# Feed-forward kernel, first product: two token groups inside the inner-dimension loop, in two PSUM banks, with one stationary tile

## The chip, the cores and the metric

The kernel runs on one core of a Trainium2 chip. The metric is the device time of one execution in microseconds, the median of several runs. One core has a matrix engine (PE in the profile, with its weight loads listed apart as PEld), a vector engine (DVE), a scalar engine (ACT), a general one (POOL), and a sync engine whose queue (SP) starts most DMAs. Each engine works through its own instructions in order; engines wait for one another by semaphores. Matrix products are accumulated in PSUM, which has eight banks here, each a tile of 128 partitions by 512 float32 numbers.

## The reference, cut to what matters

One step of a diffusion backbone with one layer, over 1280 tokens: 1024 sample tokens and 256 prompt tokens, with D = 1024 columns and an inner width of 4096 in the feed-forward part.

```python
u = rmsnorm(x, g_norm1) * (1 + sc1) + sh1
proj = u @ w_in                      # pooling, gating, q/k/v/o, gates
y_a = pool_branch(xp, ...)           # centred means, minus x, per-group linear map
y_b = sgu_branch(su, sv, ...)        # chunks of 128 positions
y_c = mlstm_branch(q, k, v, ...)     # 4 heads, forward and backward scans
merged = sum_r sigmoid(gate_r) * (y_r @ w_branch[r])
x = x + gt1 * (merged @ w_out)
u2 = rmsnorm(x, g_norm2) * (1 + sc2) + sh2
x = x + gt2 * (jnp.square(jax.nn.relu(u2 @ w_ff1)) @ w_ff2)
y = rmsnorm(x, g_final)
```

## The kernel before

**Tiling.** Tokens stand in three groups (GROUPS): group 0 and group 1 with 512 sample tokens each, group 2 with the 256 prompt tokens. A product keeps its accuracy by splitting both operands into a high and a low part and doing three matmuls per inner step: high by high, high by low, low by high. The function `dense` (L117 to L125) does so for one group of tokens: for each of eight inner steps k it issues L123 and L124, which share the weight slice `whi[:, s]` as the stationary operand, and L125 with `wlo[:, s]`. All eight steps accumulate in one PSUM tile.

**PSUM.** The eight banks are shared out between two rings of tiles: `ps_mm` (L75, 3 banks) for projections and for the first feed-forward product, and `ps_sd` (L78, 5 banks) for nearly all else: the mLSTM heads, the pooling branch's product (L683), the chunk mixing (L704) and the second feed-forward product. A tile can be written again once its last reader is done.

**What sets the order.** The program is written stage by stage, but the tile framework's scheduler places each instruction: it estimates when operands and buffers come free, and moves ready work ahead. So one stage's matmuls stand among another's, and what stands where on PE depends on the PSUM rings, too. On the chip each engine then keeps that order and only waits.

**The stages in time**, by the profile's clock: start and conditioning to about 130 us, mLSTM heads to about 451, pooling branch and the start of the gating branch to about 525, gated branch outputs and output projection to about 1240, feed-forward to the end.

**Heads and pooling.** A head's last product per token tile is `pv` (L561, L563); DVE and ACT normalise it (L566 to L577), and L580 makes `yc`. After the last head its scratch space `z` is used by the pooling branch: POOL clears parts of it (L630 to L635), for each of four channel groups (3, 2, 1, 0) a projection `xp` is copied out of PSUM (L641), windowed sums run over `z` on DVE and POOL (`winsum`, L663), are multiplied by the inverse counts (L670, L674) and reduced by `xp` (L681); then PE does `pp` (L683), and L686 and L687 split the result. The projections for `xp` and for the gating branch `su` are made by `dense` and depend on none of that. L617 normalises the rows `vn` of the gating branch, which stand in the same stretch of DVE.

**Feed-forward** (L859 to L942). Sixteen blocks `fb`, each with two inner tiles `f` of 128 of the 4096 inner columns. `ff_in(g, f)` makes the first product of one group with one inner tile (`dense` into `ps_mm`), then relu (L871) and square (L873) on ACT, square and difference (L874, L875) on DVE. `ff_out(g)` adds the block's part of the second product, per token tile and half of the columns: six matmuls (L888 to L890) into `ps_sd`, multiplied by `gt2` (L897) and added to the rows `xt` (L898) on DVE. In the last block part of these go to a temporary on DVE (L894) and are added on POOL (L895), then rows are normalised, scaled (L903) and written out (L905, L907). The weights come through `load_w` (L86): a DMA, the high part by ACT (L93), the low part by DVE (L94), with three buffers for each part.

Of the kernel before, what the change touches and what calls it, by code (L numbers as in the profile page):

```python
# [35 lines left out]
class Pinned:  # L36
    """Engine whose instructions stay in program order."""

# [11 lines left out]
def hybrid_step(  # L50
# [21 lines left out]
    def tmp(name, dt=F32):  # L72
        return tp.tile([P, 512], dt, tag="t", name=name)

    def ps_mm(name):  # L75
        return pp.tile([P, 512], F32, tag="mm", name=name, bufs=3)

    def ps_sd(name):  # L78
        return pp.tile([P, 512], F32, tag="sd", name=name, bufs=5)

# [73 lines left out]

    # RMSNorm, modulation and transpose of a group of tokens
    def norm_rows(x, n, name):
# [38 lines left out]

    # conditioning: SiLU, then shift1 and scale1 as columns
    scond = cp.tile([P, KT, 2], F32, name="scond")
# [106 lines left out]

    # gate pre-activations
    bgt = cp.tile([36, 2], F32, name="bgt")
# [110 lines left out]

    # remaining modulation rows: shares of the vector engine, summed over partitions on GpSimd
    macc = []
# [26 lines left out]

    # one mLSTM head
    knat = z[:, 0:1280].rearrange("p (c t) -> p c t", t=P)
# [144 lines left out]

    # normalised rows for the spatial gating branch
    vn = []
# [22 lines left out]

    # pooling branch
    wpt = z[:, 7200:7712].rearrange("p (g c) -> p g c", c=P)  # L620
# [69 lines left out]

    # spatial gating branch
    wst = z[:, 9216:9728].rearrange("p (g c) -> p g c", c=P)
# [30 lines left out]

    # gated branch outputs, summed
    zoff = (0, 4096, 8192)
# [41 lines left out]

    # output projection and residual
    mT = [[] for _ in range(KT)]
# [31 lines left out]
    def modulate_ff(g):  # L801
        t0, n = GROUPS[g]
        tiles = range(t0 // P, (t0 + n) // P)
        fs = small([P, 4], f"fs{g}")[:, : len(tiles)]
        V.reduce_sum(fs, fsq[:, tiles[0] : tiles[-1] + 1, :], axis=mybir.AxisListType.X)
        r = rstd_of(fs, len(tiles), f"f{g}")
        # normalised rows are made a quarter of the columns at a time, so that little room is needed
        j = 1 if g == 2 else 0
        for qt in range(4):
            xn = []  # L810
            for ii, i in enumerate(tiles):
                if ii % 2 == 0:
                    t = tmp(f"xn{i}_{qt}")
                v = t[:, (ii % 2) * 256 : (ii % 2) * 256 + 256]
                xv = xt[i][:, qt * 256 : (qt + 1) * 256]
                if ii % 2 == 0:
                    A.activation(v, xv, AF.Copy, scale=r[:, ii : ii + 1])
                else:
                    V.tensor_scalar(v, xv, r[:, ii : ii + 1], None, ALU.mult)
                xn.append(v)  # L820
            for kk in range(2):
                k = qt * 2 + kk
                ps = ps_sd(f"pt2{g}_{k}")
                for ii in range(n // P):
# [26 lines left out]

    # feed-forward
    gt2 = bcast_rows(3 * D, "gt2")
# [6 lines left out]
    for fb in range(NFF // FB):  # L860
# [4 lines left out]

        def ff_in(g, f):
            n = GROUPS[g][1]
            ps = ps_mm(f"f1_{fb}_{f}_{g}")
            dense(ps, w1[f], u2, g)
            t = tmp(f"re{f}_{g}")  # L870
            A.activation(t[:, :n], ps[:, :n], AF.Relu)  # L871
            part = split_part(f"h{f}", g)
            A.activation(part[0], t[:, :n], AF.Square)  # L873
            V.tensor_tensor(t[:, :n], t[:, :n], t[:, :n], ALU.mult)  # L874
            V.tensor_tensor(part[1], t[:, :n], part[0].bitcast(F32), ALU.subtract)  # L875
            hid[f].append(part)

# [45 lines left out]

        # a group's rows start the first block as soon as they are ready,
        # and in the last one are finished under the products of the next group
        if fb == 0:
            order = [(g, f) for g in range(3) for f in range(FB)]
        elif last:
            order = [(g, f) for f in range(FB) for g in range(2)]
            load_w2()  # L930
        else:
            order = [(g, f) for f in range(FB) for g in range(3)]
        for g, f in order:
            ff_in(g, f)
        if not last:
            load_w2()
        ff_out(0)
        if last:
            for f in range(FB):
                ff_in(2, f)  # L940
        ff_out(1)
# [103 lines left out]
```

## Time and profile before

| what | value |
|---|---|
| times of three runs | 2095.59, 2093.40, 2092.47 us |
| median | 2093.4 us |
| span of the profiled execution, first to last instruction | 2092.1 us |
| mean granted PE clock over the span | 0.993 |
| ACT busy | 581.7 us (28%) |
| POOL busy | 229.3 us (11%) |
| data moved | 142.74 MB, 68 GB/s on average |

The profile's page gives a span and no separate time for the profiled execution; the span is 1.3 us below the median of the runs and 0.4 us below the fastest. A window of the trace lists, for a stretch of time, how long each engine was busy, with the number of its instructions, the mean clock granted to PE (1.00 is full speed) and the share of DMA time. A row of the timeline gives the start, the length, engine and line, operation, output and inputs, and in brackets the idle time before it with what ended it. A PE row's length includes the pipeline's drain: where one matmul starts right behind another, the distance between two starts is what it costs.

### The profile page before, as it was taken

The numbers are of one execution on the slowest core, as the hardware profiler recorded it, in microseconds if no ns is written. First come the engines' busy times: TensorE is split into PE (matmuls) and PEld (weight loads), VectorE is DVE, ScalarE is ACT, GpSimd is POOL, SyncE is SP. The second block draws the span as 40 slices with busy tenths as digits, with TensorE's granted clock in tenths as the row PEclk, the third lists the DMA queues.
The fourth block names the chain that finished last, engine by engine and source line by source line (L and its number), as shares of the span: only waits on it lengthen the run. The fifth ranks groups of instructions, "written<-read, shape, count | busy, mean of one in ns | idle before, by whom it ended". The sixth has DMA issues, their size and how long they took to land.

```text
span 2092.1 us, 27452 instructions
## 1 busy us (share of the span) xinstructions
PE 2039.9 (98%) x11120; PEld 1758.5 (84%) x11120; DVE 1243.9 (59%) x2075; ACT 581.7 (28%) x1210; POOL 229.3 (11%) x207
## 2 busy tenths in 40 slices
PE   6999999998999999999999999999999999999996
PEld 3788888996888888888899988888888888888885
DVE  6674444458543345445253687666666666666777
ACT  6534454643111111111132431111111111111113
POOL 2000001037022222122010100000000000000004
PEclk9999999999999999999999999999999999999998
DMA  8011111124122343252141111111111111111102
GB/s 314 21 33 54 42 58 46 39 66 161 56 73 79 97 156 91 71 182 75 48 151 41 55 37 41 41 41 41 41 41 41 41 41 39 33 41 41 41 21 101
DMA packets 56479, 142.74 MB, mean 68 GB/s; under 512 B 6944, under 2 KB 12960, under 8 KB 56352
## 3 DMA queue, kind: packets, MB, share of 16 engines
q1 hardware_dynamic: 45568, 122.03, 18.6%
q10 hardware_dynamic: 7488, 11.02, 1.4%
q0 software_dynamic: 3296, 7.94, 1.3%
q8 instruction: 87, 1.43, 0.3%
q14 instruction: 40, 0.33, 0.1%
HBM read 124.67 MB, written 16.29 MB: 67 GB/s over the span
## 4 chain that ended last, share of the span: by engine, by line
PE 93%; DVE 3%; issue 1%; POOL 1%; DMA 1%; ACT 1%; SPq 0%; DVEq 0%; POOLq 0%; ACTq 0%
PE f L124 7%; PE f L123 7%; PE f L125 7%; PE f L888 7%; PE f L889 7%; PE f L890 7%; PE br L123 5%; PE br L124 5%; PE br L125 5%; PE pb L756 3%; PE pb L758 3%; PE pb L757 3%; PE po L841 2%; PE po L842 2%; PE po L843 2%
## 5 line engine op out<-in xcount | busy, mean ns | idle before, releaser
L897 DVE TENSOR_TENSOR f<-f,gt 128x512 f32<-128x512 f32 x305 | 211.1, 697 | 42.1 <-PE f L890 42.1
L898 DVE TENSOR_TENSOR z<-z,f 128x512 f32<-128x512 f32 x305 | 207.3, 684 | 7.3
L93 ACT CAST hi_f<-raw_f 128x1024 fp32r<-128x1024 f32 x63 | 64.6, 1049 | 462.7 <-PE f L889 417.4
L874 DVE TENSOR_TENSOR re<-re 128x512 f32<-128x512 f32 (+1 forms) x96 | 57.4, 599 | 165.9 <-ACT h1h L873 116.8
L751 ACT ACTIVATE sg<-br 128x512 f32<-128x512 f32 (+1 forms) x72 | 37.9, 526 | 300.8 <-PE br L125 287.6
L895 POOL TENSOR_TENSOR z<-z,fo 128x512 f32<-128x512 f32 x15 | 20.4, 1367 | 849.7 <-DVE fo L894 848.1
L871 ACT ACTIVATE re<-f 128x512 f32<-128x512 f32 (+1 forms) x96 | 50.4, 526 | 196.2 <-PE f L125 196.1
L889 PE MATMUL f<-hi_f,h0l 128*128 128x512 f32 x256 | 99.7, 390 | 0.0
L890 PE MATMUL f<-lo_f,h0h 128*128 128x512 f32 x256 | 99.6, 389 | 0.0
L888 PE MATMUL f<-hi_f,h0h 128*128 128x512 f32 x256 | 99.1, 390 | 0.0
L94 DVE TENSOR_TENSOR lo_f<-raw_f,hi_f 128x1024 fp32r<-128x1024 f32 x63 | 77.0, 1222 | 31.0 <-ACT hi_f L93 30.9
L888 PE MATMUL f<-hi_f,h1h 128*128 128x512 f32 x240 | 93.4, 389 | 0.0
L889 PE MATMUL f<-hi_f,h1l 128*128 128x512 f32 x240 | 93.4, 389 | 0.0
L436 DVE SCALAR_TENSOR_TENSOR acc<-wb,scond,acc 128x512 f32<-128x512 f32 x112 | 82.2, 791 | 18.2 <-DMA wb<-in_w_ada 18.2
L890 PE MATMUL f<-lo_f,h1h 128*128 128x512 f32 x240 | 92.7, 389 | 0.0
L443 POOL PARTITION_ALL_REDUCE acc<-acc x16 | 54.3, 3435 | 324.2 <-DVE acc L436 290.0
L765 DVE TENSOR_TENSOR sg<-pb,sg 128x512 f32<-128x512 f32 (+1 forms) x48 | 28.7, 599 | 100.8 <-PE pb L758 95.9
L763 DVE TENSOR_TENSOR z<-pb,sg 128x512 f32<-128x512 f32 (+1 forms) x24 | 14.4, 600 | 78.9 <-PE pb L758 78.9
L890 PEld LDWEIGHTS f<-lo_f,h0h 128*128 128x128 f32 x256 | 48.1, 188 | 10.0
L889 PEld LDWEIGHTS f<-hi_f,h0l 128*128 128x128 f32 x256 | 48.1, 188 | 9.3
L888 PEld LDWEIGHTS f<-hi_f,h0h 128*128 128x128 f32 x256 | 48.1, 188 | 9.3
L94 DVE TENSOR_TENSOR lo_br<-raw_br,hi_br 128x1024 fp32r<-128x1024 f32 x24 | 37.2, 1551 | 28.9 <-ACT hi_br L93 28.8
(1656 smaller groups left out, 6271.3 us busy)
## 6 DMA issues: line engine op xcount, KB each, us to landing
raw_f<-in_w_ff SPq DMA_DIRECT2D x64, 512.0 KB, 3.7
wb<-in_w_ada SPq DMA_DIRECT2D x32, 512.0 KB, 4.0
raw_br<-in_w_in SPq DMA_DIRECT2D x24, 512.0 KB, 3.6
wa<-in_w_ada SPq DMA_DIRECT2D x32, 256.0 KB, 5.4
raw_wb<-in_w_branch SPq DMA_DIRECT2D x12, 512.0 KB, 3.6
z<-in_xs SPq DMA_DIRECT2D x10, 512.0 KB, 7.2
z<-in_xs POOLq DMA_DIRECT2D x10, 512.0 KB, 4.8
out_y<-z SPq DMA_DIRECT2D x9, 512.0 KB, 2.6
```

Source lines behind the costliest of these rows:

```text
L93: A.copy(hi, raw)
L94: eng.tensor_tensor(lo, raw, hi.bitcast(F32), ALU.subtract)
L123: PE.matmul(ps[:, :n], whi[:, s], ahi, start=k == 0, stop=False)
L124: PE.matmul(ps[:, :n], whi[:, s], alo, start=False, stop=False)
L125: PE.matmul(ps[:, :n], wlo[:, s], ahi, start=False, stop=k == KT - 1)
L436: V.scalar_tensor_tensor(acc[j], wa[:, k2, :], scond[:, k, j : j + 1], acc[j], ALU.mult, ALU.add)
L756: PE.matmul(pb[:, :n], wb[0][:, s], yh, start=kc == 0, stop=False)
L888: PE.matmul(ps, hh[:, o : o + P], whi, start=f == 0, stop=False)
L889: PE.matmul(ps, hl[:, o : o + P], whi, start=False, stop=False)
L890: PE.matmul(ps, hh[:, o : o + P], wlo, start=False, stop=f == FB - 1)
L897: V.tensor_tensor(ps, ps, gt, ALU.mult)
L898: V.tensor_tensor(xt[i][:, s], xt[i][:, s], ps, ALU.add)
```

## The change

`ff_in` no longer takes one group but a tuple of groups, and no longer calls `dense`. For each inner step k it goes over the three operand pairs, and inside over the groups: with the tuple (0, 1) the same stationary slice is used twice in a row, for group 0 into one bank and for group 1 into another. In blocks 1 to 14 the order is groups (0, 1) together and then group 2, for each inner tile; in the first block the groups stay single, and in the last block (0, 1) together come first and group 2 after `ff_out(0)`, as before. So that two tiles of the first product can be open at once, `ps_mm` has four banks in place of three, and `ps_sd` four in place of five. Comments were taken out. The number and the sizes of the matmuls, and all work on the other engines, are the same.

```diff
     def ps_mm(name):
-        return pp.tile([P, 512], F32, tag="mm", name=name, bufs=3)
+        return pp.tile([P, 512], F32, tag="mm", name=name, bufs=4)
     def ps_sd(name):
-        return pp.tile([P, 512], F32, tag="sd", name=name, bufs=5)
+        return pp.tile([P, 512], F32, tag="sd", name=name, bufs=4)
...
-        def ff_in(g, f):
-            n = GROUPS[g][1]
-            ps = ps_mm(f"f1_{fb}_{f}_{g}")
-            dense(ps, w1[f], u2, g)
-            t = tmp(f"re{f}_{g}")
-            A.activation(t[:, :n], ps[:, :n], AF.Relu)
...
+        def ff_in(gs, f):
+            ps = {g: ps_mm(f"f1_{fb}_{f}_{g}") for g in gs}
+            whi, wlo = w1[f]
+            for k in range(KT):
+                s = slice(k * P, (k + 1) * P)
+                for w, part, first, end in ((whi, 0, k == 0, False), (whi, 1, False, False), (wlo, 0, False, k == KT - 1)):
+                    for g in gs:
+                        PE.matmul(ps[g][:, : GROUPS[g][1]], w[:, s], u2[k][g][part], start=first, stop=end)
+            for g in gs:
+                n = GROUPS[g][1]
+                t = tmp(f"re{f}_{g}")
+                A.activation(t[:, :n], ps[g][:, :n], AF.Relu)
...
         if fb == 0:
-            order = [(g, f) for g in range(3) for f in range(FB)]
+            order = [((0,), f) for f in range(FB)] + [((1,), f) for f in range(FB)] + [((2,), f) for f in range(FB)]
         elif last:
-            order = [(g, f) for f in range(FB) for g in range(2)]
+            order = [((0, 1), f) for f in range(FB)]
             load_w2()
         else:
-            order = [(g, f) for f in range(FB) for g in range(3)]
+            order = [(gs, f) for f in range(FB) for gs in ((0, 1), (2,))]
...
             for f in range(FB):
-                ff_in(2, f)
+                ff_in((2,), f)
```

The rings of PSUM banks serve the whole program, so the scheduler's placement changes outside the feed-forward part as well. Three places on PE show it. In these rows the output stands first, then the moving operand and the stationary one, or for `pv` and `pp` the like; a name ends in a running number, `f1_9_0_1` is block 9, inner tile 0, group 1, and `p_xp11` is the projection `xp` of channel group 1 for token group 1.

**First place: the feed-forward part, block 9**, the start of its first product. Before:

```order
L123 MATMUL f1_9_0_0_14108<-u20h0_10095,hi_f1_18_14098 128x512
L124 MATMUL f1_9_0_0_14108<-u20l0_10096,hi_f1_18_14098 128x512
L125 MATMUL f1_9_0_0_14108<-u20h0_10095,lo_f1_18_14099 128x512
L123 MATMUL f1_9_0_0_14108<-u21h0_10105,hi_f1_18_14098 128x512
L124 MATMUL f1_9_0_0_14108<-u21l0_10106,hi_f1_18_14098 128x512
L125 MATMUL f1_9_0_0_14108<-u21h0_10105,lo_f1_18_14099 128x512
L123 MATMUL f1_9_0_0_14108<-u22h0_10121,hi_f1_18_14098 128x512
```

After:

```order
L873 MATMUL f1_9_0_0_14108<-u20h0_10095,hi_f1_18_14098 128x512
L873 MATMUL f1_9_0_1_14109<-u20h1_10316,hi_f1_18_14098 128x512
L873 MATMUL f1_9_0_0_14108<-u20l0_10096,hi_f1_18_14098 128x512
L873 MATMUL f1_9_0_1_14109<-u20l1_10317,hi_f1_18_14098 128x512
L873 MATMUL f1_9_0_2_14172<-u20c_10476,hi_f1_18_14098 128x256 x2
L873 MATMUL f1_9_0_0_14108<-u20h0_10095,lo_f1_18_14099 128x512
L873 MATMUL f1_9_0_1_14109<-u20h1_10316,lo_f1_18_14099 128x512
L873 MATMUL f1_9_0_0_14108<-u21h0_10105,hi_f1_18_14098 128x512
```

Before, the tile of group 0 is filled step by step, and the tile of group 1 later; now the two tiles alternate, each stationary slice standing twice in a row, and a few matmuls of group 2 stand between them. Counted over the program, 903 pairs of neighbouring 512-column matmuls of the first product now share the stationary slice and differ in the bank; before there were 3.

**Second place: the end of the last mLSTM head**, where PE does the last `pv` tiles (`pv3_8`, `pv3_9`) among projections. Before:

```order
L123 MATMUL p_xp32_4460<-u6c_806,hi_xp3_4402 128x256
L124 MATMUL p_xp32_4460<-u6c_806,hi_xp3_4402 128x256
L561 MATMUL pv3_8_3764<-z_80,w3_2_0_3744 128x129
L561 MATMUL pv3_9_3775<-z_80,w3_2_0_3744 128x129
L563 MATMUL pv3_9_3775<-z_80,e3_2_0_3749 128x129
L125 MATMUL p_xp32_4460<-u6c_806,lo_xp3_4403 128x256
L561 MATMUL pv3_8_3764<-z_80,w3_2_1_3755 128x129
L561 MATMUL pv3_9_3775<-z_80,w3_2_1_3755 128x129
```

After:

```order
L123 MATMUL p_xp11_4708<-u3h1_683,hi_xp1_4677 128x512
L124 MATMUL p_xp11_4708<-u3l1_684,hi_xp1_4677 128x512
L561 MATMUL pv3_8_3764<-z_80,w3_2_0_3744 128x129
L561 MATMUL pv3_9_3775<-z_80,w3_2_0_3744 128x129
L561 MATMUL pv3_8_3764<-z_80,w3_2_1_3755 128x129
L563 MATMUL pv3_8_3764<-z_80,e3_2_1_3760 128x129
L563 MATMUL pv3_9_3775<-z_80,e3_2_0_3749 128x129
L561 MATMUL pv3_9_3775<-z_80,w3_2_1_3755 128x129
```

Before, the projections standing here are the third of `xp3`, channel group 3; now they are the second of `xp1`. The projections `xp2` for all three token groups, `xp1` for token group 0 and part of `xp1` for token group 1 have moved ahead of the head's end, with the rest of `xp3`: counted over the program, 83 matmuls of 512 columns and 28 of 256 more stand ahead of the last `pv3_9`.

**Third place: the pooling branch's products `pp`** of channel groups 1 and 0. Before:

```order
L683 MATMUL pp1_0_4775<-xp1_0_4706,z_80 128x512
L123 MATMUL p_su00_4958<-u2h0_419,hi_su0_4954 128x512
L124 MATMUL p_su00_4958<-u2l0_420,hi_su0_4954 128x512
L125 MATMUL p_su00_4958<-u2h0_419,lo_su0_4955 128x512
L123 MATMUL p_su00_4958<-u3h0_499,hi_su0_4954 128x512
L124 MATMUL p_su00_4958<-u3l0_500,hi_su0_4954 128x512
L125 MATMUL p_su00_4958<-u3h0_499,lo_su0_4955 128x512
L123 MATMUL p_su00_4958<-u4h0_541,hi_su0_4954 128x512
L124 MATMUL p_su00_4958<-u4l0_542,hi_su0_4954 128x512
L125 MATMUL p_su00_4958<-u4h0_541,lo_su0_4955 128x512
L683 MATMUL pp1_1_4784<-xp1_1_4733,z_80 128x512
L683 MATMUL pp1_2_4793<-xp1_2_4760,z_80 128x256
```

After:

```order
L125 MATMUL p_su10_5072<-u7h0_577,lo_su1_5069 128x512
L683 MATMUL pp2_0_4642<-xp2_0_4570,z_80 128x512
L683 MATMUL pp2_1_4651<-xp2_1_4597,z_80 128x512
L683 MATMUL pp2_2_4660<-xp2_2_4624,z_80 128x256
L683 MATMUL pp1_0_4775<-xp1_0_4706,z_80 128x512
L683 MATMUL pp1_1_4784<-xp1_1_4733,z_80 128x512
L683 MATMUL pp1_2_4793<-xp1_2_4760,z_80 128x256
L683 MATMUL pp0_0_4905<-xp0_0_4839,z_80 128x512
L683 MATMUL pp0_1_4914<-xp0_1_4866,z_80 128x512
L683 MATMUL pp0_2_4923<-xp0_2_4893,z_80 128x256
```

Before, projections `su` stand between the products of the channel groups; now those of groups 2, 1 and 0 follow one another with nothing between, and the projections stand ahead of them. Counted up to the last `pp0` tile, 32 matmuls of 512 columns and 24 of 256 of the `su` projections more stand ahead of it than before. From the mixing product `mx2_0` on, some 15 us of PE work later, the same work stands ahead of each tile in both programs up to the last feed-forward block.

In that last block all matmuls of group 2's first product now stand ahead of `f2_15_2_0`, the second product of token tile 2, and the tiles `f2_15_0_0` to `f2_15_1_1` are filled by turns and finish together: 7 matmuls of 512 and 45 of 256 columns more stand ahead of the end of `f2_15_0_0`; before, `f2_15_0_0` to `f2_15_1_1` finish one after another, and group 2's first product starts behind `f2_15_2_0`.

More of the change, by code (lines that the diff above doesn't have):

```diff
@@ L864, in hybrid_step @@
             w1.append(load_w(w_ff1[fb * FB + f], f"f1_{fb * FB + f}"))
-        def ff_in(g, f):
-            n = GROUPS[g][1]
-            ps = ps_mm(f"f1_{fb}_{f}_{g}")
-            dense(ps, w1[f], u2, g)
-            t = tmp(f"re{f}_{g}")
-            A.activation(t[:, :n], ps[:, :n], AF.Relu)
[L872 to L876, printed above, removed]
+        def ff_in(gs, f):
[10 more added lines that the diff above has]
+                A.activation(t[:, :n], ps[g][:, :n], AF.Relu)
+                part = split_part(f"h{f}", g)
+                A.activation(part[0], t[:, :n], AF.Square)
+                V.tensor_tensor(t[:, :n], t[:, :n], t[:, :n], ALU.mult)
+                V.tensor_tensor(part[1], t[:, :n], part[0].bitcast(F32), ALU.subtract)
+                hid[f].append(part)
         def ff_out(g):
@@ L926, in hybrid_step @@
         if fb == 0:
-            order = [(g, f) for g in range(3) for f in range(FB)]
+            order = [((0,), f) for f in range(FB)] + [((1,), f) for f in range(FB)] + [((2,), f) for f in range(FB)]
         elif last:
-            order = [(g, f) for f in range(FB) for g in range(2)]
+            order = [((0, 1), f) for f in range(FB)]
             load_w2()
         else:
-            order = [(g, f) for f in range(FB) for g in range(3)]
-        for g, f in order:
-            ff_in(g, f)
+            order = [(gs, f) for f in range(FB) for gs in ((0, 1), (2,))]
+        for gs, f in order:
+            ff_in(gs, f)
         if not last:
```

## The prediction

> **What bounds the kernel now.** I read the page from the top: busy shares, the slices of the span, the chain that ended last.
>
> ```profile
> PE 2039.9 (98%) x11120; PEld 1758.5 (84%) x11120; DVE 1243.9 (59%) x2075; ACT 581.7 (28%) x1210; POOL 229.3 (11%) x207
> PE   6999999998999999999999999999999999999996
> PEclk9999999999999999999999999999999999999998
> PE 93%; DVE 3%; issue 1%; POOL 1%; DMA 1%; ACT 1%; SPq 0%; DVEq 0%; POOLq 0%; ACTq 0%
> ```
>
> PE is busy 98% of 2092.1 us and carries 93% of the chain. Only three slices in forty fall below nine tenths: the first, the tenth and the last, each 52 us long. So a change that leaves the matmuls as they are can act in two ways alone: on the distance between matmuls, or on those few stretches where PE stands still. The windows show them:
>
> ```profile
> 400.00:450.00 50.00, 50.00 (x379) 47.82 (x378) 23.37 (x68) 28.80 (x102) 4.11 (x7) 1.00 0.13 46
> 450.00:500.00 50.00, 43.60 (x222) 36.34 (x220) 41.12 (x38) 15.72 (x34) 41.78 (x34) 1.00 0.31 103
> 500.00:550.00 50.00, 47.90 (x248) 39.34 (x249) 37.33 (x52) 12.85 (x19) 12.41 (x16) 0.93 0.38 130
> 1300.00:2040.00 740.00, 740.00 (x3558) 625.11 (x3557) 509.81 (x756) 142.24 (x218) 0.00 (x0) 1.00 0.13 38
> 2040.00:2092.10 52.10, 34.56 (x174) 28.89 (x172) 41.68 (x71) 16.31 (x46) 25.63 (x25) 0.87 0.25 101
> ```
>
> The columns are the window and its length, the busy time of PE, PEld, DVE, ACT and POOL, PE's clock, DMA share and GB/s. In the feed-forward part, which the change is written for, PE is never idle (740.00 of 740.00) at full clock. In the pooling stage it stands still for 6.4 + 2.1 = 8.5 us, in the last window for 17.5.
>
> **Term 1: the paired matmuls, 0.** The first product has 903 pairs that share the stationary slice and differ in the bank. The trace of before holds such a neighbour, in the second block:
>
> ```profile
> 1231.13 0.39 PE L123 MATMUL f<-u20h,hi_f 128*128 128x512 f32 x1
> 1231.35 0.39 PE L124 MATMUL f<-u20l,hi_f 128*128 128x512 f32 x1
> 1231.36 0.19 PEld L123 LDWEIGHTS f<-u20h,hi_f 128*128 128x128 f32 x1
> 1231.58 0.39 PE L123 MATMUL f<-u20h,hi_f 128*128 128x512 f32 x1
> 1422.40 0.39 PE L123 MATMUL f<-u20h,hi_f 128*128 128x512 f32 x1
> 1427.84 0.28 PE L123 MATMUL f<-u20c,hi_f 128*128 128x256 f32 x1
> 1430.71 0.40 PE L123 MATMUL f<-u20h,hi_f 128*128 128x512 f32 x1
> ```
>
> The matmul at 1231.35 is the last of this turn on group 0, that at 1231.58 the first on group 1: same slice, other bank. Its weights are still loaded again (1231.36), under the running matmul, and it starts 0.23 us after its neighbour. 1231.13 to 1231.35, same slice and same bank, is 0.22. The last three rows enclose one tile each of 24 matmuls, within one bank: 5.44 us for 512 columns, 226.7 ns a matmul, and 2.87 for 256 columns, 119.6 (below, 0.2267 and 0.120). Two sizes give a line: (226.7 − 119.6)/256 = 0.418 ns per column and 12.5 ns that do not depend on columns. Were the reload the cause of those 12.5 ns and saved in each pair, the gain would be 903 × 12.5 = 11.3 us; a change of bank that cost as much would lose as much. Neither shows in the rows at 1231, so I take 0; of the ends, −11 stays in the range, while for +11 no row speaks and it falls in with rival C.
>
> The Trainium skill, "TensorE: Matmul & The Clock Gate", section "Step-by-step: what each phase is for", says that loads and matmuls are separate instructions so that a slice can be loaded once and used by many matmuls. By that this change would remove 903 loads; the trace does not agree, since the second matmul of the same slice has a load of its own in the rows above. By the rule the sum would be 11 us lower.
>
> **Term 2: banks and DVE in the feed-forward part, 0.** With four banks instead of five for the second product, PE can come to a bank that DVE still reads.
>
> ```profile
> L897 DVE TENSOR_TENSOR f<-f,gt 128x512 f32<-128x512 f32 x269 | 186.4, 697 | 35.4 <-PE f L890 35.4
> L898 DVE TENSOR_TENSOR z<-z,f 128x512 f32<-128x512 f32 x269 | 183.0, 684 | 6.5
> L94 DVE TENSOR_TENSOR lo_f<-raw_f,hi_f 128x1024 fp32r<-128x1024 f32 x54 | 66.0, 1222 | 29.1 <-ACT hi_f L93 29.1
> ```
>
> A tile costs DVE 0.697 + 0.684 = 1.38 us and PE 6 × 0.2267 = 1.36. In a run of such tiles both keep step. With four banks PE comes back to a bank after three more tiles, 4.08 us; of these 1.38 are the drain, and 2.70 remain for other DVE work ahead of it, with five banks 4.06. A weight split (1.22) and one pair of squares fit into 2.70. Over the stretch DVE is busy 509.81 of 740, 69%, and matmuls of the first product still stand between runs of tiles. So 0; if the cover fails, by one weight split less the remaining slack, about 1 us per block or 15 us in all. That is a rival below, of which +4 enters the range.
>
> **Term 3: the pooling stage, +9.** This is no part of the feed-forward code, yet the rings of banks serve the whole program, and the rows in the second and third place of the change show the projections moved. 83 matmuls of 512 columns and 28 of 256 more stand ahead of the last `pv3_9`: 83 × 0.2267 + 28 × 0.120 = 22.2 us. PE is full there (50.00 of 50.00 before 450), so the head ends 22.2 us later. That alone costs nothing, since this work is then gone from later. But a chain starts at the head's end which needs almost no PE:
>
> ```profile
> 451.02 0.53 POOL L632 MEMSET z<- 128x512 f32 x1 [12.60 <-PE pv L561]
> 452.55 2.33 DVE L94 TENSOR_TENSOR lo_xp<-raw_xp,hi_xp 128x1024 fp32r<-128x1024 f32 x1 [0.69 <-ACT hi_xp L93]
> 460.94 9.06 DVE L617 TENSOR_SCALAR vn<-vn,rs_v 128x512 f32<-128x512 f32 x10 [2.99 <-POOL rs_v L130]
> 470.63 1.22 DVE L94 TENSOR_TENSOR lo_su<-raw_su,hi_su 128x1024 fp32r<-128x1024 f32 x1
> 472.20 9.43 DVE L663 TENSOR_TENSOR z<-z 128x1920 f32<-128x1920 f32 x4
> 483.34 3.42 DVE L681 TENSOR_TENSOR xp<-z,xp 128x512 f32<-128x512 f32 x2
> 516.36 1.83 DVE L681 TENSOR_TENSOR xp<-z,xp 128x512 f32<-128x512 f32 x2
> 520.48 1.02 PE L683 MATMUL pp<-xp,z 128*128 128x512 f32 x2
> 521.57 1.45 PE L683 MATMUL pp<-xp,z 128*128 128x512 f32 x4
> ```
>
> POOL's clearing waits 12.60 us for the head's `pv`: the scratch space is shared, so nothing of the pooling branch can begin earlier. From 451.0 to the end of the last L681 at 518.2 it is 67.2 us, and DVE has the same work in it after the change, in nearly the same order. Out of it goes the split of `xp` weights, now done earlier (2.33), while splits of `su` weights trade places, three for three: 64.9. The last L681 then ends at 473.2 + 64.9 = 538.1, and the last `pp0` follows it by about 1.9 us at 540.0, against 521.57 + 1.45 = 523.0 before: 17.0 later. Up to there PE has more done by 32 × 0.2267 + 24 × 0.120 = 10.1 us. The rest, **6.9 us**, is lost, because the matmuls that stood between the `pp` have run ahead and nothing is left to fill the waits. Clock comes on top:
>
> ```profile
> 496.00:502.00 6.00, 0.70 (x6) 0.50 (x5) 6.00 (x6) 2.18 (x4) 6.00 (x8) 0.94 0.42 153
> 502.00:508.00 6.00, 5.90 (x13) 3.64 (x14) 5.76 (x6) 2.92 (x5) 3.95 (x9) 0.50 0.55 178
> ```
>
> After an idle stretch PE ran six microseconds at half clock and lost 5.90 × 0.5 = 2.95 us. With longer and more idle stretches one more such stretch is likely: between nothing and two of them, 0 and 5.9; I take 2.2, below one, as few matmuls stand right behind the waits. Together +9.1. The low end is 0, if DVE's chain runs 9 us shorter in its new surroundings; the high end 6.9 + 5.9 + 1.2 (one more split) = 14.
>
> **Term 4: the end, +2.** In the last block DVE's first final product moves back:
>
> ```profile
> 2043.91 1.28 DVE L894 TENSOR_TENSOR fo<-f,gt 128x512 f32<-128x512 f32 x2
> 2074.54 0.50 PE L888 MATMUL f<-hi_f,h0c 128*128 128x512 f32 x1 [1.64 <-DVE fo L894]
> 2075.80 0.40 PE L890 MATMUL f<-f2l,h1c 128*128 128x512 f32 x1
> 2085.47 2.74 DVE L903 SCALAR_TENSOR_TENSOR z<-z,rs_x,gf 128x512 f32<-128x512 f32 x4 [0.48 <-POOL rs_x L130]
> 2043.90:2088.30 44.40, 30.66 (x157) 25.66 (x155) 40.38 (x70) 15.08 (x44) 25.63 (x25) 0.89 0.25 100
> 2060.42 0.75 DVE L874 TENSOR_TENSOR re<-re 128x256 f32<-128x256 f32 x2
> 2061.69 0.41 DVE L875 TENSOR_TENSOR h0c<-re,h0c 128x256 fp32r<-128x256 f32 x1
> DVE f L897 <- PE f L890: 1.5, 1, 1.5
> DVE fo L894 <- PE f L890: 0.4, 1, 0.4
> ```
>
> PE ends at 2076.2, DVE at 2088.2, so DVE sets the end: 40.38 busy in 44.40. The woven tiles and group 2's first product ahead of `f2_15_2_0` put 7 matmuls of 512 and 45 of 256 columns more ahead of the end of `f2_15_0_0`: 7 × 0.2267 + 45 × 0.120 = 7.0 us. DVE starts its run 7.0 late, has done group 2's squares (0.75 + 2 × 0.41 = 1.6) before it, and can close up at most its 4.0 of idle time: 7.0 − 1.6 − 4.0 = +1.4 at best, +5.4 at worst. I take +2, nearer to the closed end: half of DVE's idle time are the two waits for PE in the last rows, and a late DVE finds those inputs ready. Range 0 to +5.
>
> **The sum** is 0 + 0 + 9 + 2 = 11 on the profiled execution's span of 2092.1. The span is 1.3 below the median of the runs, 2093.4, so the median becomes 2104.5.
>
> **The rivals.**
> *A, the pair is cheaper.* If the second matmul of a pair lost its 12.5 ns, 11.3 us go and 2093 is left: not slower. It decides from (11 − 4)/903 = 8 ns per pair. Against it speak the rows at 1231; for it only that they are few. Chance 0.06, and 0.04 that it comes without the loss of term 3, near 2084.
> *B, the pooling chain closes up,* because DVE and POOL, freed of projections' splits, are quicker by 9 us: 2095.5. For it: DVE idles 2.99 us ahead of L617, in the chain itself. Against it: it is busy 41.12 of 50. Chance 0.11.
> *C, DVE falls behind in every block* for lack of the fifth bank, 1 us in 15 blocks: 2119. For it: 1.38 against 1.36 per tile. Against it: DVE's 31% of idle time. Chance 0.07.
> *D, clock.* The same page of the Trainium skill, section "A second HAM failure mode: psum-queue depth-cycling", tells of a kernel that cycled through banks and fell again and again to half clock between bursts. In this kernel it would need gaps; one stretch as at 502 in each block would cost 2.95 × 15 = 44 us, 2148. The clock is 1.00 through 740 us of bank changes at the end of every tile. Chance 0.02.
>
> ```profile
> PE pp L683 <- DVE xp L681: 5.4, 1, 5.4
> ```
>
> This wait, now the only one of note at L683, is the place where the forecast shows first.
>
> **How the numbers follow.** The forecast has 0.67 (2096 to 2113), A 0.06, A without term 3 0.04, B 0.11, C 0.07, D 0.02, and 0.03 is left to unnamed gains. About what a measurement of this kernel can tell from no change is 0.2%, 4.2 us. Faster: 0.04 + 0.03 = 0.07. Same: A, B and 0.02 of the forecast's low end, 0.19. Slower: 0.65 + 0.07 + 0.02 = 0.74. The range takes in A and B below and the two high ends above (2093.4 + 14 + 5 = 2112.4, with a little of C): 2092 to 2114; outside lie 0.16.
>
> **What would show it.** Right: rows of paired matmuls 0.2267 apart with a load before each; POOL's L632 starting near 473; the last `pp0` near 540, with waits for L681 of 10 us more in the windows 450 to 550; the first final product on DVE some 16 us later than 2043.9 by the clock (9 from the front, 7 from the order), and no idle PE from 1300 to 2040. Wrong: a spacing near 0.214 in pairs (A), `pp0` before 534 (B), waits for DVE at the second product's first matmul in each block (C), a granted clock below 1.00 there (D).

## The result, and the profile after

The changed kernel takes 2118.08 us (median of four runs, 2116.54 to 2119.52), the kernel before 2092.97: the ratio is 1.0119, with a 95% interval of 1.0105 to 1.0133. It is slower, as forecast, but by 25 us instead of 11, and outside the range, which ended at 2114. The span of the profiled execution is 2115.1 us against 2092.1, 23.0 more.

The page of the changed kernel, with the same four rows as before:

```profile
PE 2047.0 (97%) x11120; PEld 1758.8 (83%) x11120; DVE 1243.7 (59%) x2075; ACT 574.1 (27%) x1210; POOL 225.6 (11%) x207
PE   6999999998899999999999999999999999999995
PEclk9999999999899999999999999999999999999998
PE 72%; DVE 2%; issue 0%; POOL 0%; ACT 0%; DVEq 0%; POOLq 0%; ACTq 0%
```

The slices show the same picture with one spot more: the tenth and the eleventh slice (about 476 to 582 us) now both lie below nine tenths, and in the eleventh the clock dips, too. PE is busy 7 us longer for the same matmuls, in part because more of them run at half clock. The shares of the last row add up to 74% only, 100% before, so the chain was not followed through the whole span and the two rows are not to be compared. Then the windows, with the columns as before:

```profile
450.00:500.00 50.00, 50.00 (x284) 43.77 (x283) 30.49 (x52) 17.62 (x50) 18.34 (x21) 1.00 0.23 77
500.00:550.00 50.00, 32.70 (x124) 21.52 (x123) 43.08 (x37) 15.23 (x25) 33.98 (x33) 0.83 0.47 166
1300.00:2040.00 740.00, 740.00 (x3552) 623.68 (x3551) 500.77 (x757) 128.05 (x208) 0.00 (x0) 1.00 0.12 38
2040.00:2115.00 75.00, 53.00 (x243) 42.54 (x241) 57.46 (x92) 22.48 (x56) 26.01 (x25) 0.88 0.20 78
```

From 450 to 550 PE stands still for 17.3 us (8.5 before), at a clock of 0.83 in the second half. From 1300 to 2040 it is never idle, as before. At the end it is idle for 22.0 us (17.5 before). The paired matmuls themselves, in the timeline of the changed kernel (start, length, then a row for two neighbours):

```profile
1399.70 0.61 PE L873 MATMUL f<-u25h,lo_f 128*128 128x512 f32 x2
1400.15 0.62 PE L873 MATMUL f<-u26h,hi_f 128*128 128x512 f32 x2
1400.61 0.62 PE L873 MATMUL f<-u26l,hi_f 128*128 128x512 f32 x2
```

A pair starts every 0.45 or 0.46 us, two matmuls at 0.227 each. Neither the shared slice nor the change of bank shows in it. The page still counts one weight load per matmul (PEld x11120): a slice that is used twice in a row is loaded twice.

**Where the 23.0 us arise.** The same tile can be found in both traces, and the PE work that stands ahead of it is known from the order of the matmuls. The difference of the two starts, less the difference of that work, is what PE has lost up to there, by waiting or by a lower clock:

| up to | lost | the stretch alone |
|---|---|---|
| end of the last mLSTM head | 1.6 us | 1.6 |
| mixing product `mx2_0`, behind the pooling stage | 14.3 | 12.7 |
| first feed-forward tile | 14.1 | −0.2 |
| last tile of block 14 | 15.6 | 1.5 |
| first final product of the last block | 16.2 | 0.6 |
| end of the span | 23.0 | 6.8 |

So two places carry it, those of terms 3 and 4, and the feed-forward blocks, which the change was written for, only 1.5 us. One execution differs from another already in the starting stage, before the first head's first `pv` at about 170 us: with the order of matmuls of the kernel before, the profiled executions below had lost −2.4 to +3.3 us by then, the changed kernel's −0.5. What is lost behind that point differs less from run to run.

### The profile page after: what moved, and what is told of

It is laid out like the page before. It is cut to its first block, busy times and chain, and to the rows that moved or that the text cites. A ratio compares the mean times of both kernels' runs of the same rounds, so it can differ in the third digit from the quotient of the medians.

```text
span 2115.1 us, 27468 instructions
## 1 busy us (share of the span) xinstructions
PE 2047.0 (97%) x11120; PEld 1758.8 (83%) x11120; DVE 1243.7 (59%) x2075; ACT 574.1 (27%) x1210; POOL 225.6 (11%) x207
## 4 chain that ended last, share of the span: by engine, by line
PE 72%; DVE 2%; issue 0%; POOL 0%; ACT 0%; DVEq 0%; POOLq 0%; ACTq 0%
PE f L873 21%; PE f L895 7%; PE f L894 7%; PE f L896 7%; PE br L123 5%; PE br L124 5%; PE br L125 5%; PE pb L756 3%; PE pb L757 3%; PE pb L758 3%; PE po L843 2%; PE po L841 2%; PE po L842 2%; DVE z L909 1%; PE p_su L123 1%; PE p_su L125 1%
## 5 line engine op out<-in xcount | busy, mean ns | idle before, releaser
L903 DVE TENSOR_TENSOR f<-f,gt 128x512 f32<-128x512 f32 x305 | 209.8, 696 | 127.0 <-PE f L896 126.9
L894 PE MATMUL f<-hi_f,h0h 128*128 128x512 f32 x256 | 99.9, 391 | 1.9 <-DVE fo L900 1.0
L894 PE MATMUL f<-hi_f,h1h 128*128 128x512 f32 x240 | 87.4, 389 | 0.0
L894 PEld LDWEIGHTS f<-hi_f,h0h 128*128 128x128 f32 x256 | 48.0, 188 | 12.5 <-DVE fo L900 1.8
```

What stands on the lines that cost most here:

```text
L894: PE.matmul(ps, hh[:, o : o + P], whi, start=f == 0, stop=False)
L903: V.tensor_tensor(ps, ps, gt, ALU.mult)
```

## The experiments

All variants are of one of the two kernels. "Lost" below is worked out as in the table; for the work moved, matmuls were counted in the order, at 0.2267 and 0.120 us. "Lost in the pooling stage" is from the end of the last head to `mx2_0`.

**1 to 4: rings and pairs apart.** A first set takes the change to pieces. Rings only, on the kernel before:

```diff
-        return pp.tile([P, 512], F32, tag="mm", name=name, bufs=3)
+        return pp.tile([P, 512], F32, tag="mm", name=name, bufs=4)
-        return pp.tile([P, 512], F32, tag="sd", name=name, bufs=5)
+        return pp.tile([P, 512], F32, tag="sd", name=name, bufs=4)
```

> The kernel before with only the PSUM rings changed (four banks for mm, four for sd), nothing paired. Theory (the rings move the projections ahead of the last head and empty the pooling stage of filler; the last block's order delays DVE): PE's work ahead of the last pv3_9 is 405.6 us as in the changed kernel (383.5 before), ahead of f2_15_0_0's end 1961.1 (1958.2 before), so +14 from the pooling stage and +3 from the end: about 2110 us. Rival (the alternation of two banks itself costs the time): no pairs here, so about 2093 us.

Pairs only: the changed kernel with these two lines as before.

> The changed kernel with the rings of before (three banks for mm, five for sd), pairs kept. Theory: PE's order up to the pooling stage is that of before, so 0 there; pairs cost 0.1 us per block, 1.4; the end of f2_15_0_0 stands behind 4.1 us more PE work than before: about 2098.5 us, with the pooling stage's POOL clearing at 451 and the last pp0 near 523. Rival (alternation costs it): about 2118 us, with PE's excess spread over the feed-forward part.

The changed kernel with single groups in the last block:

```diff
-            order = [((0, 1), f) for f in range(FB)]
+            order = [((g,), f) for f in range(FB) for g in range(2)]
```

> The changed kernel with the last block's first product not paired, the rest as changed. Theory: pooling stage +14, pairs +1.4, end of f2_15_0_0 behind 3.6 us more PE work than before instead of 7.0: about 2113 us, 3.4 less than the changed kernel on the trace's span. Rival for the tail (one bank fewer for the second product paces the end, whatever the order of the first product): as the changed kernel, about 2117.

The same edit on the pairs-only kernel:

> The changed kernel with the rings of before and the last block not paired: pairs in blocks 1 to 14 alone. Theory: 0 in the pooling stage, pairs +1.4, end +0.5: about 2095 us, not to be told from before. Rival (alternation costs it): about 2116 us.

| kernel | banks mm, sd | time | ratio to before, interval | lost in the pooling stage | first final product on DVE | from there to the end |
|---|---|---|---|---|---|---|
| before | 3, 5 | 2093.40 beside these runs | | | 2043.9 | 44.3 |
| changed | 4, 4 | 2118.08 | 1.0119, 1.0105 to 1.0133 | 12.7 | 2066.9 | 44.5 |
| rings only | 4, 4 | 2112.38 | 1.0094, 1.0079 to 1.0109 | 13.0 | 2063.8 | 44.5 |
| pairs only | 3, 5 | 2096.99 | 1.0021, 1.0011 to 1.0030 | 0.2 | 2047.8 | 44.6 |
| changed, last block single | 4, 4 | 2115.62 | 1.0110, 1.0095 to 1.0125 | 13.2 | 2064.0 | 46.5 |
| pairs in blocks 1 to 14 | 3, 5 | 2093.64 | 1.0003, 0.9993 to 1.0012 | 0.0 | 2047.6 | 44.0 |

The alternation itself costs nothing: with the old rings and the last block single the time is that of the kernel before, though 744 pairs are left in the order. The pairs-only program has 772, and its windows read like those of before, row by row:

```profile
450.00:500.00 50.00, 43.59 (x222) 36.34 (x220) 41.12 (x38) 15.69 (x33) 40.85 (x33) 1.00 0.32 103
1300.00:2040.00 740.00, 740.00 (x3558) 625.14 (x3557) 510.18 (x757) 132.07 (x216) 0.00 (x0) 1.00 0.13 38
```

With the rings alone 19 of the 25 us are there although the code of that kernel pairs nothing. The last column says what the end is: from DVE's first final product to the end of its last operation it takes 44.0 to 46.5 us in all six, however the matmuls stand; the end moves with that first product. In the pairs-only kernel it stands behind 4.1 us more PE work than before and comes 3.9 us later. The 3.6 us by which the pairs-only kernel is slower than the kernel before are thus the order of the last block, not the pairs. In the fourth kernel the profiled execution lost 3.3 us in the starting stage, which the median of its ten runs doesn't show; that column's 2047.6 has it in. In the third the first product came 2.9 us earlier than in the changed kernel, but the run took 2.0 longer, so that on the spans only 0.8 was saved, 2.5 on the medians.

**5, 6 and 8: the rings the other way.** If only the work left in the pooling stage counts, two banks for `mm` should help: `bufs=2` and `bufs=6`, on the kernel before, on the changed one, and on the kernel of the seventh experiment.

> The kernel before, nothing paired, with two banks for mm and six for sd: the rings moved the other way. Theory (what counts in the pooling stage is the PE work left between the last head's end and pp0, against the DVE chain of about 70 us): the work left is 444.5 - 363.2 = 81 us here, 60 before, 48 in the changed kernel, so the chain is covered and the stall of 8.5 us with its half clock goes: POOL's clearing near 431, pp0 without waits, about 2083 us. Rival (any departure from three and five banks costs, since two mm banks leave PE waiting for each projection's copy): at 2093 or above, with new waits for ACT in the head stage.

> The changed kernel with two banks for mm and six for sd: a pair now takes the whole mm ring. Theory: pooling stage as in the run with two and six banks unpaired (about -10), but the tile after each pair must wait for both relus unless matmuls of the second product stand between; 28 pairs with 0 to 1 us each, and the end of f2_15_0_0 behind 4.5 us more work: 2088 to 2115 us. Rival (pairs need a bank to spare in any case): above 2118.

> Two and six banks, unpaired, and the final scaling of six tiles moved from DVE as in the run on the tail. Theory: the two gains lie at different places and add, about 2078 us. Rival (one is hidden by the other): no faster than the better of the two.

All three missed. Two and six took 2105.84 us unpaired (1.0057, 1.0045 to 1.0070), 2122.68 paired (1.0135, 1.0121 to 1.0149), 2110.40 with the edit for the end (1.0079, 1.0065 to 1.0093). Yet the pooling stage did what the theory says: unpaired it loses 4.0 us less than before, though not the 10 that were expected. The time went elsewhere, as PE's list of waits shows (engine and line, what it waits for, us in all, times, longest), with one row of the paired kernel last:

```profile
PE pt_u L168 <- DVE z L182: 8.4, 2, 7.9
PE pp L683 <- DVE xp L681: 4.6, 2, 2.7
PE po L841 <- ACT po L848: 4.0, 4, 2.5
```

```profile
PE f L873 <- ACT re L877: 7.9, 16, 0.9
```

The second row is the pooling stage itself, 4.6 us where it was 5.4. In the starting stage the waiting transposes `pt_u` start when they did before (70.6 us; 70.4), as their rows come no earlier, but with 22 projection matmuls (5.0 us) fewer done: work that filled this wait now stands behind it. In the output projection, whose tiles lie in `mm`, PE waits for the last reader of a bank. And a pair that fills both banks makes the next tile wait for its relus, 16 times for half a microsecond. The direction in the pooling stage held, the sum for the kernel did not: each of the other stages has a price in banks of its own, which the expectations left out.

**9 and 10: the chain in the pooling stage.** Ten row scalings that stand in DVE's chain go to ACT, in both kernels:

```diff
-        V.tensor_scalar(vn[i], vn[i], r[:, i : i + 1], None, ALU.mult)
+        A.activation(vn[i], vn[i], AF.Copy, scale=r[:, i : i + 1])
```

> The kernel before with the ten row scalings vn taken from DVE (9.06 us in one run, between the last head's end and the pooling branch) and done by ACT. Theory (the pooling stage is set by the DVE chain from the last head's end to pp0, and PE stalls for what the chain is longer than the work left): the chain gets 5 to 9 us shorter, the work left is 445.4 - 383.5 = 62 us, so most of the stall of 8.5 us and its half clock go: 2083 to 2089 us. Rival (POOL's window sums or the waits for the inverse counts set the chain): 2093 us, with DVE idle ahead of L663 instead.

> The changed kernel with the ten row scalings vn on ACT. Theory: PE's order is that of the changed kernel, the chain 5 to 9 us shorter, and with 48 us of work left all of that counts: 2109 to 2113 us. Rival (POOL or DMA set the chain, or the loss of the changed kernel does not lie in this chain): 2118 us.

2090.88 us (0.9987, 0.9978 to 0.9995) and 2115.25 (1.0103, 1.0088 to 1.0119): both 2 to 3 us better than without the edit, in the right place (the pooling stage loses 2.6 us less than in the kernel before, and 8.6 instead of 12.7 in the changed one), but half of what was expected or less. The timeline of the second of them shows where the rest went. On ACT:

```profile
483.88 4.41 ACT L617 ACTIVATE vn<-vn,rs_v 128x512 f32<-128x512 f32 x7
488.20 1.95 ACT L617 ACTIVATE vn<-vn,rs_v 128x512 f32<-128x512 f32 x3
491.41 1.05 ACT L668 COPY z<-z 128x1024 f32<-128x1024 f32 x1
492.49 1.14 ACT L647 COPY z<-xp 128x512 f32<-128x512 f32 x2
```

and on DVE:

```profile
487.94 2.59 DVE L115 TENSOR_TENSOR yc<-yc,yc 128x256 fp32r<-128x256 f32 x1
492.49 6.85 DVE L663 TENSOR_TENSOR z<-z 128x1920 f32<-128x1920 f32 x3 [1.97 <-ACT z L668]
```

and on POOL:

```profile
482.41 7.83 POOL L663 TENSOR_TENSOR z<-z 128x1216 f32<-128x1216 f32 x3
```

ACT's copy L668 is a link of the same chain, and the scalings now stand ahead of it there. But POOL's window sums, which L668 copies, end at 490.24, and DVE's `yc`, whose transfer ACT starts ahead of it, at 490.53, no earlier than the scalings on ACT (490.15). Three paths end there together, and L668 starts at 491.41: by these rows, taking the scalings off ACT as well would gain less than 1 us at this place. The first of DVE's window sums starts 15.5 us after POOL's clearing (476.95) instead of 19.7: 4.2 us of the 9 are gained. The rival of both expectations, that POOL's sums set the chain, with DVE idle ahead of L663, is thus true in part.

**11: the fourth bank kept apart.** The changed kernel with three banks for `mm`, four for `sd` and one of its own for group 1's tile:

```diff
+    def ps_x(name):
+        return pp.tile([P, 512], F32, tag="x1", name=name, bufs=1)
...
-            ps = {g: ps_mm(f"f1_{fb}_{f}_{g}") for g in gs}
+            ps = {g: (ps_x if g == 1 else ps_mm)(f"f1_{fb}_{f}_{g}") for g in gs}
```

> The changed kernel, but the fourth bank of the first product stands apart and serves only group 1's tile of the feed-forward part: three banks for mm, one of its own, four for sd. Theory (the fourth mm bank moved the projections; the tail is the first final product's place in PE's order): the work left between the last head's end and pp0 is 446.2 - 388.3 = 58 us as against 60 before and 48 in the changed kernel, so about +2 in the pooling stage instead of +14; the last block is that of the changed kernel, +7, and the feed-forward part +2: about 2104 us, DVE's run from its first final product again 44 us. Rival (four sd banks make the loss in the pooling stage): 2116 to 2118 us.

2116.34 us (1.0105, 1.0088 to 1.0122): the rival's time, but not for the rival's reason. The pooling stage loses 1.7 us, as the theory said. Up to the end of the heads 11.7 us are lost ahead of it, 10 of them in one place, between the first and the last `pv` of the third head. Window 350 to 400 of the kernel before, and of this one:

```profile
350.00:400.00 50.00, 49.04 (x414) 48.66 (x413) 24.23 (x70) 31.39 (x96) 6.49 (x4) 1.00 0.19 60
```

```profile
350.00:400.00 50.00, 41.91 (x333) 40.37 (x332) 21.44 (x64) 31.80 (x102) 5.05 (x4) 0.93 0.12 40
```

Its list of waits has

```profile
PE th L581 <- ACT z L580: 5.0, 1, 5.0
```

PE stands 5.0 us at a head's transpose `th` and runs at half clock behind it. So what the two rings do can be said more exactly than before. From the first `pv` to the mixing products, which leaves the starting stage out, PE lost 12 to 15 us in all five kernels with four `sd` banks and the old vn scaling, and at most 0.2 in the four with five (and three for `mm`). The fourth `mm` bank only decides where: with four the projections run ahead through the heads (22.2 us of work more at the end of the last), and are then missing in the pooling stage; with three they run ahead by 4.8 us, and a head waits. Why the order puts the head's `th` there was not followed further, and a kernel with three and four banks and the eighth left unused was not run. So this is shown for the orders that this scheduler made of these rings, not as a rule for any order.

**7, 12 and 13: the end.** If DVE's run sets the end, taking work from it should shorten it. Six of the twenty final scalings L903 went to ACT and POOL:

```diff
+                        if hf == 1 and i < 6:
+                            A.activation(xt[i][:, s], xt[i][:, s], AF.Copy, scale=r[:, 0:1])
+                            G.tensor_tensor(xt[i][:, s], xt[i][:, s], gf[hf], ALU.mult)
+                        else:
```

> The kernel before, with the final scaling of the right half of token tiles 0 to 5 taken from DVE and done by ACT (times r) and POOL (times gf). Theory (DVE's run from its first final product sets the end, whatever PE does): six DVE operations of about 1.2 us go, 7 us, the end moves up by 4 to 7 us: about 2088 us. Rival (PE's second product in four or five banks paces the end): no change, 2093 us.

2096.35 us (1.0013, 1.0004 to 1.0022): no gain, if anything a loss; the run from the first final product grew to 47.7 us. The other way round, all 15 additions that POOL does in the last block went to DVE (`if last and (...)` became `if False`):

> The kernel before with the last block's additions all on DVE, none on POOL. Theory (DVE's operations at the end are stretched while POOL adds): the final scalings fall from 1.07 to about 0.70 us each (20 x 0.37 = 7.4 us less), 15 additions of 0.68 us come on (10.3 us more): about +3, 2096 us. Rival (the stretch of DVE's final scalings has nothing to do with POOL): scalings stay at 1.07, +10, 2103 us.

2091.86 us (0.9994, 0.9984 to 1.0003), with 15 operations more on DVE: not told apart from the kernel before, and not the 3 us slower that were expected. From the first final product to the end it takes 42.2 us. Groups of the window from 2040 on, first the kernel before, then with six scalings moved to POOL, then with nothing of this on POOL (last columns: count, busy time, mean ns of one, idle before):

```profile
L903 DVE SCALAR_TENSOR_TENSOR z<-z,rs_x,gf 128x512 f32<-128x512 f32 x20 | 20.5, 1068 | 1.5 <-POOL rs_x L130 1.5
L894 DVE TENSOR_TENSOR fo<-f,gt 128x512 f32<-128x512 f32 x15 | 10.0, 682 | 0.4 <-PE f L890 0.4
```

```profile
L907 DVE SCALAR_TENSOR_TENSOR z<-z,rs_x,gf 128x512 f32<-128x512 f32 x14 | 17.6, 1281 | 2.6 <-POOL rs_x L130 2.3
L894 DVE TENSOR_TENSOR fo<-f,gt 128x512 f32<-128x512 f32 x15 | 10.0, 683 | 0.4 <-PE f L890 0.4
```

```profile
L903 DVE SCALAR_TENSOR_TENSOR z<-z,rs_x,gf 128x512 f32<-128x512 f32 x20 | 14.0, 745 | 1.2 <-POOL rs_x L130 1.2
L897 DVE TENSOR_TENSOR f<-f,gt 128x512 f32<-128x512 f32 x20 | 13.5, 691 | 0.7 <-PE f L890 0.7
```

The scaling takes 745 ns without POOL's additions, 1068 with them and 1281 with still more on POOL; six fewer saved DVE only 2.9 us. The products that read PSUM (L894, L897) stay at 0.68 to 0.69 in all three. So work moved to POOL came back as longer DVE operations, and work taken back from it costs DVE next to nothing: it is busy for 40.3 us of its run with the 15 additions and for 40.4 without. The Trainium skill, "SBUF — State Buffer", section "Who interferes with whom", says that a DVE operation with two inputs in SBUF contends with a POOL operation that reads SBUF, because its second input comes through a read interface that the two share. These rows agree, for the scaling has both inputs there and the product one in PSUM. The same edit on the changed kernel:

> The changed kernel with the last block's additions all on DVE, none on POOL. Theory (the last block costs what its first final product comes later, and DVE's run from there is as long as in the kernel before with the same edit, 42.2 us): the pooling stage's loss stays, the end comes 2 us earlier than in the changed kernel, 2116 us. Rival (in the changed kernel PE's waits for one of only four banks set the end, so that freeing banks later, since the sum into the rows is now on DVE, costs more): 2120 us or above, with a run well over 44 us.

2115.23 us (1.0103, 1.0087 to 1.0119), and 41.0 us from the first final product to the end: the four banks do not lengthen it. The rival for the end falls.

**14: a version that beats both.** The vn scalings on ACT and the additions on DVE, three and five banks, nothing paired:

> The kernel before with the row scalings vn on ACT and the last block's additions all on DVE: three and five banks, nothing paired. Theory: two places, two gains that add, 2.4 us from the pooling stage and 1 to 2 from the end: about 2089.5 us, 0.2% below the kernel before. Rival (both lie within the noise of the chip): 2093 us.

2088.95 us; the ratio to the kernel before is 0.9976, 0.9967 to 0.9986. The two small gains add, 2.4 us each by the medians of their sets (the second not clear of the noise by itself) and 4.8 together, as their places lie apart.

## Why the prediction was wrong

The direction and the two places were right; the range was not, as both terms were too small. Span against span the sum was +11, measured +23.0.

*Term 1, the paired matmuls, 0:* right. The rows at 1231 were enough, and rival A with its 11 us is out: pairs alone leave the time as it was. Between 1300 and 2030 us, in the pairs-only kernel, the second matmul of a pair starts 226.7 ns after the first on average; in the kernel before, a 512-column matmul of the first product takes 227.0.

*Term 2, banks and DVE in the blocks, 0:* nearly right, +1.5 over 14 blocks, with no wait at all from 1300 to 2040. It does not come from the pairs alone, for the pairs-only kernel shows none of it, nor from the rings alone, with 0.4. It comes with pairs and four `sd` banks together (1.5 also with the bank apart), and sits for the most part in the second product's matmuls, 0.8 ns each. What causes it stays open. Rivals C and D did not occur.

*Term 3, the pooling stage, +9:* right mechanism, wrong size; the stretch lost 12.7 and what lies ahead of it 1.6. The step that failed is the length of the chain. The prediction let it shrink from 67.2 to 64.9 us by the `xp` split that leaves it, and took everything else at its old duration; measured, it grew to 68.4. The changed kernel's timeline has:

```profile
474.71 0.53 POOL L632 MEMSET z<- 128x512 f32 x1 [14.75 <-PE pv L561]
480.23 10.34 DVE L617 TENSOR_SCALAR vn<-vn,rs_v 128x512 f32<-128x512 f32 x10 [2.38 <-POOL rs_v L130]
494.40 6.53 DVE L663 TENSOR_TENSOR z<-z 128x1920 f32<-128x1920 f32 x3 [1.51 <-ACT z L668]
499.27 3.57 POOL L663 TENSOR_TENSOR z<-z 128x1120 f32<-128x1120 f32 x1
500.85 3.07 DVE L94 TENSOR_TENSOR lo_su<-raw_su,hi_su 128x1024 fp32r<-128x1024 f32 x1
542.41 0.68 DVE L681 TENSOR_TENSOR xp<-z,xp 128x512 f32<-128x512 f32 x1
541.89 4.63 PE L683 MATMUL pp<-xp,z 128*128 128x512 f32 x6 [3.52 <-DVE xp L681]
```

and, from PE's list of waits, what was 5.4 us before; below it, another row of the list of the kernel before:

```profile
PE pp L683 <- DVE xp L681: 15.4, 4, 6.7
```

```profile
PE pp L683 <- issue: 3.1, 1, 3.1
```

The clearing came at 474.7 (forecast: 473.2), the last L681 ended at 543.1 (538.1), the last `pp0` at 541.89 + 4.63 = 546.5 (540.0). From clearing to `pp0` it is 71.8 us, and 72.0 in the kernel before: it did not shrink at all, and rival B, a chain that closes up, is out. The split did leave: from clearing to L617 it is 5.5 us instead of 9.9. But from there to the first window sum on DVE it is 14.2 instead of 11.3, and from that to the end of the last L681 48.7 instead of 46.0. Rows grew in their new company: the ten L617 from 9.06 to 10.34, one `su` split from 1.22 to 3.07. The long split stands beside a window sum of POOL (499.27), while POOL was waiting for a transfer beside the split of 1.22 (470.63 in the kernel before); that looks like the effect at the end of the kernel (runs 7 and 12), but no run tested it here. And the last six `pp` ran at half clock, 4.63 us against 2.5.

By kind of loss: PE's idle time from 450 to 550 grew by 8.8 us where the forecast had 6.9. At half clock, as the clock by windows has it, PE worked for 12.6 us in three stretches (from 510, 531 and 541) instead of 6.0 in one, and half of the difference, 3.3 us, is lost where the forecast had 2.2. The wait for L681 grew by the forecast 10 us to the tenth, which is partly luck: the prediction called this wait the only one of note at L683 and passed over the 3.1 us above, which are part of the 8.5 us of idle time before.

A better estimate was at hand: 72 us from clearing to `pp0` as it was, less the work left in it, 59.9 us before and 47.7 after, gives 12.2 more lost, without any detail of the chain.

*Term 4, the end, +2:* right mechanism, wrong size. The first final product came 7.0 us later by the order, as counted, but nothing of it was won back. DVE's timeline in the changed kernel, at the beginning, in the middle and at the end of its run:

```profile
2066.92 1.29 DVE L900 TENSOR_TENSOR fo<-f,gt 128x512 f32<-128x512 f32 x2 [2.22 <-PE f L896]
2082.77 1.28 DVE L880 TENSOR_TENSOR re<-re 128x256 f32<-128x256 f32 x2
2109.96 1.42 DVE L909 SCALAR_TENSOR_TENSOR z<-z,rs_x,gf 128x512 f32<-128x512 f32 x2 [0.73 <-POOL rs_x L130]
```

In the windows, DVE's run reads so, and its final scalings in the groups so:

```profile
2066.90:2111.40 44.50, 26.33 (x105) 19.89 (x104) 41.90 (x69) 15.08 (x44) 26.01 (x25) 0.84 0.26 107
```

```profile
L909 DVE SCALAR_TENSOR_TENSOR z<-z,rs_x,gf 128x512 f32<-128x512 f32 x20 | 22.3, 1153 | 1.6 <-POOL rs_x L130 1.5
```

The run takes 44.5 us, as before. The step "has done group 2's squares before it" failed: they stand at 2082.77, in the middle of the run, as they did at 2060.42 before; the prediction did not take DVE's new order there into account. The idle time did close a little, from 4.0 us (44.40 − 40.38) to 2.6 (44.50 − 41.90), but DVE's operations grew by as much: the final scalings alone by 20 × (1.153 − 1.068) = 1.7 us. The value was chosen at the favourable end of +1.4 to +5.4, and the measured 6.8 lies above the other.

Of the range: its upper end, 2114, has the high ends of terms 3 and 4 both in (14 and 5) and still fell 4 us short of the median. The spans differ by 23.0, the medians by 25.1; the 2 us between them are within the scatter of the runs.

## What to carry to other kernels

A ring of PSUM banks belongs to the whole program: moving one bank to where a new loop needs it cost 12 to 15 us in stages that the edit never touched, and at most 1.5 in the loop itself. Where a chain on other engines starts late and PE waits for its end, compare two numbers, the chain's length and the PE work left beside it; take the length from a whole stretch of the trace rather than by subtracting single rows. At a tail set by one engine, count what its first instruction waits for, and take no credit for idle time that it may close up.

## What the runs showed of the hardware that was not expected

DVE's final scalings, with both inputs in SBUF, took 0.75 us without POOL's additions, 1.07 beside them and 1.28 beside more work on POOL, so taking six of them off DVE saved it 2.9 us instead of the 7 expected. Part of the gain of the best version (2.3 of 5.8 us on the spans, 2088.6 to 2086.3 and 2092.1 to 2086.3) comes from giving DVE more to do and POOL less. And a change of bank between matmuls, with the same stationary slice or another, had no price in the 772 pairs of the pairs-only kernel, and using the slice twice in a row no gain: 227 ns for 512 columns with the pair as without.
